# Values' products of two heads on the two halves of the array, and low halves of weights moved from GpSimd to VectorE

## The chip, the cores and the metric

One core of a Trainium2 chip runs the whole kernel. The time is that of the device for one execution, in microseconds (us), from several runs; the profile is of one more execution. TensorE multiplies matrices (its weight loads are shown as an engine of their own, PEld), VectorE (DVE) and ScalarE (ACT) work on vectors, GpSimd (POOL) does too, and SyncE (SP) issues most of the DMAs.

## The reference

A token sequence (256 tokens, width 1024, float32) goes through two layers of a first block and one layer of a second. Each layer of the first block is a gated feed-forward network, a mixer and a second feed-forward network, with residual sums:

```
x = x + 0.5 * swiglu(rmsnorm(x, ffn1_norm[l]), ffn1_wg[l], ffn1_wu[l], ffn1_wd[l])
h = rmsnorm(x, mix_norm[l]) @ w_in[l]
h_a, h_b, h_c = jnp.split(h, [A_COLS, A_COLS + B_COLS], axis=-1)
o = concatenate([mla_mixer(h_a, ...), nsa_mixer(h_b, ...), diff_mixer(h_c, ...)])
x = x + o @ w_out[l]
x = x + 0.5 * swiglu(rmsnorm(x, ffn2_norm[l]), ffn2_wg[l], ffn2_wu[l], ffn2_wd[l])
```

The mixer has six heads of latent attention (mla), six of sparse attention with three parts each (compressed blocks, selected, window; nsa) and four of differential attention (diff). A head has 64 columns of values. The second block projects the normed residual to z, xBC, dt and three streams of a short convolution, runs a state-space scan and the convolution, projects back, and ends in a mixture of 16 experts.

## The kernel before

**Precision in two halves.** Weights arrive in float32 in a tile `st`. `split` makes of each unit two pieces, and of each piece a high half `wh` (a rounded copy, by ScalarE, line 167) and a low half `wl = st - wh` (a subtraction, line 168). Its argument `lo` says for either piece who subtracts: "v" is VectorE, "p" is GpSimd. `LOW`, and a small table in `w_in_groups`, name the units with a "p". The activations are split in the same way (`xhl`, `uhl`, `ohl`, `hx`), and each product is three: high by high, low by high, high by low. Plain float32 products appear in the trace as two matmul records each.

**The order of work.** The program is written in the order of the formulas, with explicit orders where it matters (`ORDER` in the mixers: w for units of w_in, mp, np, dp for the preparation of the three kinds of heads, m, n, d for the heads, df for the end of diff; `PART2` for the second block). A planner at build time then sets the order of instructions on each engine from its own costs; each engine takes its instructions strictly in that order, and the semaphores are the planner's. `behind(i)` queues the instructions of a block that run on `i`'s engine behind `i`.

**The mixer.** After the last feed-forward product, `after` makes for each of four banks the operand `xhl` (lines 268, 269) and the sums of squares `sq` (lines 281 to 288). `_mixer` puts the sum over partitions on TensorE (`pss`), computes the inverse root `r`, and multiplies by the units of w_in. `mla_prepare` norms the latent vectors (`rq`, `ckvn`), transposes them (`ckvt`, `cqt`), and builds keys (`knope`, two heads at a time, side by side in 512 columns of 64 partitions) and queries. In `nsa_prepare` a small network compresses keys and values: h1, and from it `kcmp` and `vcmp`. A head then is: scores into a bank S, a softmax on VectorE and ScalarE (rows scaled on GpSimd or VectorE), transposes of the three blocks of the weights (`ptp`, copied to `PT`), and `pv`, the product with the values into a bank O. Two heads share a bank of O: the even head writes partitions 0 to 63, the odd one 64 to 127, so each product uses 64 of the array's 128 columns (`128*64` in the trace). An nsa head has three such products: selected (`hV`), compressed (`vcmp`, 15 rows) and window. At the end `wo` projects with eight products, each in a bank W, and two additions to `xT`.

**The second block.** `z_blocks` multiplies by z's columns, `norms` gives the two inverse roots as rows `rb`, `u_operand` makes the operand `uhl` from `xT` (three instructions for each k: u on VectorE, high half on ScalarE, low half on VectorE), `z_gates` applies the gate, `residual_norm` scales `xT`. Then `proj` multiplies by the units d, b0 to b3, x0 to x3 and those of the short convolution, and `conv` follows on ScalarE and VectorE.

**The experts** are computed in pairs of two: the products `gate`, `up` and `y` of one expert fill columns 0 to 63 of the array and those of the other 64 to 127, issued in turn.

Of the kernel before, what the change touches and what calls it, by code (L numbers as in the profile page):

```python
# [34 lines left out]
         "h0 s1 s1 g0 s1 s2 s2 n0 c1 h1 s2 s3 g1 n1 s3 c2 h2 g2 s3 "  # L35
         "| c3 h3 p5 g3 n2 y a w6 t0 t1 p7 t2 w0 n3 t3 % w1 p4 w5 w2 w4 p5 w3 w7")

LOW = {k: "pp" for k in ["d", "b0", "b1", "b2", "b3", "x0", "x1", "x2", "x3", "w6", "w1", "w3"]
       + [(1, 0, 0, 1), (1, 0, 1, 0)]}
LOW.update({k: "vp" for k in ["h3", "g2"]})  # L40
ORDER = "w01 w5 w2 mp m0 m1 w8 w3 w4 w6 np w7 dp m2 m3 d0 d1 n0 n1 d2 d3 n2 n3 n4 n5 m4 df m5"

# [1 line left out]
class Block:  # L44
# [272 lines left out]
    def _ffn(self, l, which, xops, after, extra):  # L317
# [27 lines left out]
        def gu(g, units):  # L345
            ps = []
            if g == 0 and not finish:

                ws = [w for u in units for w in self.split(u, "n")]
                ps = [self.bank(tag, "gu") for tag in "BBCC"]  # L350
                for k, i in ([(k, i) for k in range(4) for i in range(4)]
                             + [(k, i) for i in range(4) for k in range(4, KD)]):
                    self.mm2(ps[i], ws[i][0][:, k], ws[i][1][:, k], xhl[:, k], k == 0, k == KD - 1)
                return ps
            for i, u in enumerate(units):
                for f, (wh, wl) in enumerate(self.split(u, "n", LOW.get((which, l, g, i), "vv"))):
                    p = self.bank("BC"[i], "gu")
                    ps.append(p)
                    if finish and g == 0:

                        o = p[:, 0:T]
                        for n, (w, x) in enumerate(((wh, xh), (wh, xl), (wl, xh))):
                            for k in range(KD):
                                self.mm(p[:, T:2 * T] if n == 1 else o, w[:, k], x[:, k], n == k == 0, n == 2 and k == KD - 1)
                        continue
                    for k in range(KD):
                        self.mm2(p, wh[:, k], wl[:, k], xhl[:, k], k == 0, k == KD - 1)
            return ps
# [21 lines left out]
            return hx  # L390

        def down(g, hx, u):
            w = self.split(u, "k", LOW.get((which, l, g, 2), "vv"))
            for b in range(4):
                for j in range(2):
                    o = acc[b][:, j * T:(j + 1) * T]
                    c = (2 * b + j) * 128
                    for k in range(2):
                        wh, wl = w[k]
                        self.mm3(o, wh[:, 0, c:c + 128], wl[:, 0, c:c + 128], hx[:, k, 0], hx[:, k, 1],  # L400
                                 g == 0 and j == 0 and k == 0, g == NG - 1 and j == 1 and k == 1)
                if g == NG - 1:
                    xv = self.xT[:, 2 * b:2 * b + 2].rearrange("p j t -> p (j t)")
                    nc.vector.scalar_tensor_tensor(xv, acc[b], 0.25, xv, op0=OP.mult, op1=OP.add)  # L404
                    after(b)
# [107 lines left out]
    def _mixer(self, l, xops, after):  # L513
# [76 lines left out]

        def w_in_groups(ids):

            ws = [self.split(units[i], "k", {2: "pp", 3: "pp", 4: "vp", 5: "vp"}.get(i, "vv")) for i in ids]
            ps = [self.bank(tags.pop(0) if tags else "W", "win") for _ in ids]
            for k0 in range(KD):
                for k, i, t in ([(k0, i, t) for i in range(len(ids)) for t in range(2)] if len(ids) > 1 else
                                [(k, 0, k0) for k in range(KD)] if k0 < 2 else []):
                    w, p, n = ws[i], ps[i], units[ids[i]][2]
                    o = p[:, t * 256:t * 256 + n]
                    ts = slice(t * 128, (t + 1) * 128)  # L600
                    first = t == 0 and k == 0
                    last = t == 1 and k == KD - 1
                    wh, wl = (v[:, k % 4] for v in w[k // 4])
                    self.mm(o, xh[:, k, ts], wh, first, False)
                    self.mm(o, xh[:, k, ts], wl, False, False)
                    self.mm(o, xl[:, k, ts], wh, False, last)
            for i, p in zip(ids, ps):
                for dst, d, c, m in groups[i][1]:
                    for t in range(2):
                        src = p[:, t * 256 + c:t * 256 + c + m]  # L610
                        if isinstance(d, tuple):

                            o = dst[:, t, 0:384].rearrange("p (u c) -> p u c", c=64)[:, d[0] // 64::2][:, 0:d[1]]
                            src = src.rearrange("p (u c) -> p u c", c=64)
                        else:
                            o = dst[:, t, d:d + m]
                        ACT(o, src, scale=r[:, t:t + 1])


        def mla_prepare():  # L620
# [44 lines left out]
            for h in range(0, 6, 2):  # L665
                p = self.bank("S", "knope")
                for i in range(2):
                    self.mm(p[0:64, i * T:(i + 1) * T], wukv[:, h + i, 0:64], ckvT, i == 0, True)
                ACT(KT[0:64, h:h + 2], p[0:64].rearrange("p (i t) -> p i t", i=2))
                p = self.bank("T", "qtp")  # L670
                for i in range(2):
                    for t in range(2):
# [6 lines left out]
        def transposes(blocks, name):  # L679

            p = self.bank("T", name)
            n = len(blocks) * 128
            for i, b in enumerate(blocks):
                tr(p[:, i * 128:(i + 1) * 128], b, ident)
            s = ap.tile([128, 384], F32, name="PT", tag="PT", bufs=4)
            return p, s, n

        def store_o(c, p):
            ACT(oh[:, c], p)
            nc.vector.tensor_sub(ol[:, c], p, oh[:, c].bitcast(F32))  # L690

        opair = {}

        def pv(h, c0, pt, v, first, last):

            if h % 2 == 0 and first:
                opair[c0] = self.bank("O", "opair")
            p = opair[c0]
            o = p[(h % 2) * 64:(h % 2) * 64 + 64]
            self.mm(o[:, 0:256], v[0], pt[:, 0:256], first, False)  # L700
            self.mm(o[:, 128:256], v[1], pt[:, 256:384], False, last)

        def softmax(s, P, segs, gate=None, low=None):

# [34 lines left out]
        def mla_head(h):  # L739
# [4 lines left out]
            scale_rows(P, SEGS, softmax(s, P, SEGS), "m")  # L744
            p, pt, n = transposes(blocks(P), "ptp")
            (nc.vector.tensor_copy if h % 2 else nc.scalar.copy)(pt, p[:, 0:n])
            pv(h, h // 2, pt, [vm[:, t, h * 64:(h + 1) * 64] for t in range(2)], True, True)
            if h % 2:
                store_o(h // 2, opair[h // 2][:, 0:256])


        def nsa_prepare():
# [24 lines left out]
            for i in range(2):  # L777
# [4 lines left out]
            p, p2 = self.bank("T", "kcmp"), self.bank("S", "vcmp")  # L782
            vcmp = ap.tile([16, 128], F32, name="vcmp", tag="vcmp")
            for g in range(2):
                self.mm(p[g * 64:(g + 1) * 64, 0:15], w2[0:64], h1[0:64, 1, g * 15:(g + 1) * 15])
                self.mm(p2[0:15, g * 64:(g + 1) * 64], h1[64:128, 1, g * 15:(g + 1) * 15], w2[64:128], g == 0, True)
# [6 lines left out]
            for g in range(2):  # L793
                ACT(ks[g * 64:(g + 1) * 64, g, 0:15], p[g * 64:(g + 1) * 64, 0:15], scale=0.5)
            ACT(vcmp[0:15], p2[0:15, 0:128], scale=0.5)
# [11 lines left out]
            for g in range(2):  # L807
                q = slice(g * 64, (g + 1) * 64)
                nc.vector.tensor_copy(ks[q, g, 16:16 + T], p3[q, 0:256])
                nc.vector.tensor_copy(kw[q, g], p3[q, 256:512])  # L810

            th = ap.tile([128, 2, 18], F32, name="gth", tag="gth")
            nc.scalar.activation(th, hV[:, :, 384:402], AF.Tanh, scale=0.5)
# [10 lines left out]
        def nsa_head(h):  # L824
# [19 lines left out]
                tr(p2[0:16, t * 128:(t + 1) * 128], P[:, 384 + t * 16:400 + t * 16], ident)  # L844
            nc.vector.tensor_copy(cpt, p2[0:16, 0:T])
            vc = slice(128 + g * 64, 192 + g * 64)
            pv(h, 3 + h // 2, pt, [hV[:, t, vc] for t in range(2)], True, False)
            o = opair[3 + h // 2]
            self.mm(o[(h % 2) * 64:(h % 2) * 64 + 64, 0:256], vcmp[0:15, g * 64:(g + 1) * 64], cpt[0:15], False, False)
            s = self.bank("S", "S")  # L850
            scores(s, qt, kw[:, g], kw[:, g, 0:128])
            P = ap.tile([128, 384], F32, name="P", tag="P", bufs=6)
# [4 lines left out]
            pv(h, 3 + h // 2, pt, [hV[:, t, vc] for t in range(2)], False, True)  # L857
            if h % 2:
                store_o(3 + h // 2, o[:, 0:256])


# [86 lines left out]
        KO = [int(c) for c in "01345672"]  # L948
        wo = [self.cols(a["w_out"][l], (b * 256, b * 256 + 256)) for b in range(4)]
        for b in range(4):  # L950
            for j, (wh, wl) in enumerate(self.split(wo[b], "n", {}.get(b, "vv"))):
                p = self.bank("W", "wo")
                for k in KO:
                    self.mm2(p, wh[:, k], wl[:, k], ohl[:, k], k == KO[0], k == KO[7])
                xv = self.xT[:, 2 * b + j]
# [66 lines left out]
    def _part2(self, xops):  # L1022
# [80 lines left out]
        def u_operand():  # L1103
            for k in range(KD):
                u = ap.tile([128, T], F32, name="u", tag="q", bufs=4)
                nc.vector.scalar_tensor_tensor(u, self.xT[:, k], self.gfm[:, k:k + 1], rb[:, 1], op0=OP.mult, op1=OP.mult)
                ACT(uh[:, k, NM:], u)
                nc.vector.tensor_sub(ul[:, k, NM:], u, uh[:, k, NM:].bitcast(F32))  # L1108

        def residual_norm():  # L1110
            for k in range(KD):
# [282 lines left out]
        def run():  # L1394
            parts = decays()
            for name in steps:
                k, i = name[0], int(name[1:] or 0)
                if k == "z":
                    zs = z_blocks([int(c) for c in name[1:]])
                    if len(zs[0]) == 1:  # L1400
                        z_gates(*zs)
                elif k == "u":
                    norms()
                    u_operand()
                    z_gates(*zs)
                elif k == "r":
                    residual_norm()
                elif k == "d":
                    next(parts)
                elif k == "b":  # L1410
# [468 lines left out]
```

## Time and profile before

| | |
|---|---|
| median of 3 runs | 1592.82 us (1591.33 to 1594.35) |
| the profiled execution | 1591.45 us; its span, from first to last instruction, 1589.7 us |
| granted TensorE clock, mean | 0.984 |
| first feed-forward network of layer 0 | to 204 us |
| mixer of layer 0 | from 204 to some 350 us |
| mixer of layer 1 | from some 740 to 905 us |
| second block without experts | from 1089 to some 1340 us |

An engine is busy while it executes; TensorE's records overlap, so the time that a product holds the engine is read from start to start. A clock of 1.0 is 2.4 GHz and 0.5 is 1.2 GHz; a window between the two had some of each. In a row, `out<-in` names the tiles.

### The profile page before, as it was taken

Reading aid. Unit: us, or ns where it says so; the run is one execution under the profiler, and the core shown is the slowest. Engines: PE = TensorE matmul, PEld = TensorE weight load, DVE = VectorE, ACT = ScalarE, POOL = GpSimd, SP = SyncE. Lnnn points to the kernel's source line nnn. Section 1 sums busy time; section 2 is a strip of 40 time slices with the busy share of each in tenths; the row PEclk is TensorE's granted clock in tenths of the full one; section 3 lists DMA queues with packets and bytes.
Section 4 is the critical chain, followed back from the end, with each engine's and each line's share of the span. In section 5 each row is a group of like instructions: output and inputs, shape, how many; then the busy total and the mean of one; then the engine's idle time right before and its main releaser. Section 6 shows DMA issues by size and latency. Waiting matters only on the chain. (4 is left out here: it accounts for less than half of the span.)

```text
span 1589.7 us, 25210 instructions
## 1 busy us (share of the span) xinstructions
PE 1527.9 (96%) x9842; PEld 1266.7 (80%) x9842; DVE 1046.6 (66%) x1988; ACT 733.9 (46%) x1385; POOL 170.7 (11%) x174
## 2 busy tenths in 40 slices
PE   7999989999999999998999999999799999999996
PEld 6999988768999989998887799999799987444342
DVE  7777774868677786778467687778798875221122
ACT  5455455645554554455556455456554443010111
POOL 3000031330000000001115000001620122000000
PEclk9999999999999999999999999999899999999999
DMA  7756644205565555555440356555443479799993
GB/s 239 223 187 192 186 133 146 81 27 184 178 195 186 186 185 187 186 186 166 132 147 1 107 188 197 194 181 190 152 133 107 153 299 350 290 396 392 393 394 125
DMA packets 223557, 308.91 MB, mean 194 GB/s; under 512 B 20908, under 2 KB 167608, under 8 KB 223432
## 3 DMA queue, kind: packets, MB, share of 16 engines
q1 hardware_dynamic: 223128, 306.71, 57.8%
q8 instruction: 79, 1.29, 0.3%
q10 hardware_dynamic: 304, 0.53, 0.1%
q14 instruction: 46, 0.38, 0.1%
HBM read 306.16 MB, written 1.05 MB: 193 GB/s over the span
## 5 line engine op out<-in xcount | busy, mean ns | idle before, releaser
L167 ACT ACTIVATE wh<-st 128x1024 fp32r<-128x1024 f32 (+1 forms) x382 | 400.1, 1060 | 355.4 <-PE gu L99 116.8
L168 DVE TENSOR_TENSOR wl<-st,wh 128x1024 fp32r<-128x1024 f32 (+1 forms) x340 | 413.2, 1226 | 207.0 <-ACT wh L167 200.1
L99 PE MATMUL gu<-xhl,wh 128*128 128x512 f32 (+1 forms) x1440 | 492.1, 391 | 3.9 <-ACT wh L167 2.2
L99 PE MATMUL gu<-xhl,wl 128*128 128x256 f32 x1408 | 388.3, 279 | 0.0
L99 PEld LDWEIGHTS gu<-xhl,wh 128*128 128x128 f32 x1440 | 267.3, 189 | 63.1 <-ACT wh L167 3.5
L99 PEld LDWEIGHTS gu<-xhl,wl 128*128 128x128 f32 x1408 | 263.5, 189 | 0.1
L99 PE MATMUL acc<-hx,wh 128*128 128x256 f32 x1408 | 252.1, 281 | 0.0
L99 PEld LDWEIGHTS acc<-hx,wh 128*128 128x128 f32 x1408 | 216.2, 188 | 1.7
L168 POOL TENSOR_TENSOR wl<-st,wh 128x1024 fp32r<-128x1024 f32 (+1 forms) x42 | 102.6, 2461 | 1015.0 <-ACT wh L167 772.3
L99 PE MATMUL acc<-hx,wl 128*128 128x256 f32 x704 | 196.9, 281 | 0.0
L99 PE MATMUL proj<-uhl,wh 128*128 128x272 f32 (+2 forms) x592 | 131.0, 311 | 8.3 <-DVE uhl L1108 6.1
L99 PEld LDWEIGHTS acc<-hx,wl 128*128 128x128 f32 x704 | 132.6, 188 | 0.0
L99 PE MATMUL win<-wh,xhl 128*128 128x256 f32 (+1 forms) x576 | 111.1, 291 | 0.2 <-DVE xT L404 0.2
L99 PEld LDWEIGHTS proj<-uhl,wh 128*128 128x128 f32 x592 | 98.5, 196 | 13.7 <-DVE uhl L1108 6.8
L99 PE MATMUL proj<-uhl,wl 128*128 128x272 f32 (+2 forms) x328 | 96.5, 294 | 0.0
L99 PEld LDWEIGHTS win<-wh,xhl 128*128 128x128 f32 x576 | 93.5, 198 | 1.8 <-issue 1.1
L99 PE MATMUL win<-wl,xhl 128*128 128x256 f32 (+1 forms) x288 | 84.7, 294 | 0.0
L388 ACT ACTIVATE hx<-up 128x512 fp32r<-128x512 f32 x44 | 27.8, 632 | 94.3 <-DVE up L387 94.3
L99 PEld LDWEIGHTS proj<-uhl,wl 128*128 128x128 f32 x328 | 64.0, 195 | 0.2
L723 POOL TENSOR_SCALAR P<-P,mx 128x128 f32<-128x128 f32 (+2 forms) x88 | 54.3, 633 | 84.1 <-DVE mx L716 68.0
L99 PEld LDWEIGHTS win<-wl,xhl 128*128 128x128 f32 x288 | 56.9, 198 | 2.9 <-issue 2.7
L1776 DVE SCALAR_TENSOR_TENSOR ys<-y,rc,ys 128x512 fp32r<-128x512 f32 x16 | 11.7, 749 | 67.2 <-ACT ys L1593 66.8
(522 smaller groups left out, 2243.1 us busy)
## 6 DMA issues: line engine op xcount, KB each, us to landing
st<-ffn_wg SPq DMA_DIRECT2D x44, 1024.0 KB, 5.4
st<-ffn_wu SPq DMA_DIRECT2D x44, 1024.0 KB, 5.4
st<-ffn_wd SPq DMA_DIRECT2D x44, 1024.0 KB, 4.9
st<-w_in SPq DMA_DIRECT2D x36, 1024.0 KB, 5.4
st<-w_out SPq DMA_DIRECT2D x16, 1024.0 KB
mf<-expert_w_gate SPq DMA_DIRECT2D x25, 512.0 KB, 9.4
mf<-expert_w_down SPq DMA_DIRECT2D x21, 512.0 KB, 10.7
mf<-expert_w_up SPq DMA_DIRECT2D x18, 512.0 KB, 11.2
```

Source lines behind the costliest of these rows:

```text
L99: return self.nc.tensor.matmul(out, lhsT, rhs, start=start, stop=stop, skip_group_check=True)
L167: hi = self.nc.scalar.activation(hl[0], src, AF.Copy)
L168: sub = (self.nc.gpsimd if lo[i] == "p" else self.nc.vector).tensor_sub(hl[1], src, hl[0].bitcast(F32))
L388: nc.scalar.activation(hh, up, AF.Copy)
L723: (nc.gpsimd if key + str(i) in "c0 c1 c2 d0 d1 m0 w0 w1".split() else nc.vector).tensor_scalar(P[:, d], P[:, d], r[:, i:i + 1], None, op0 ...
L1776: V.scalar_tensor_tensor(yl, py[half], rc[:, 1:2], yh.bitcast(F32), op0=OP.mult, op1=OP.subtract)
```

## The change

- The product with the values is no longer issued with each head: `pv` puts the head's `PT` aside, and behind the odd head `pv_pair` issues both heads' products, first both of 256 columns, then both of 128, to the two column halves in turn. The compressed products of an nsa pair follow the selected ones. The bank O is taken by the odd head. `PT` has five buffers for four.
- `knope` puts two heads on the two column halves (partitions 0 to 63 and 64 to 127), and two copies take them out, one on ScalarE, one on VectorE.
- `kcmp` and `vcmp` move behind the transposes of queries and keys.
- `LOW` keeps b3, x0 to x3 ("pp") and h3, g2 ("vp"). The low halves of d, b0 to b2, w1, w3, w6, of a gate and an up unit at the start, and of six pieces of w_in in each mixer go from GpSimd to VectorE: 30 of 42.
- `wo` takes its banks from W and S in turn.
- In the second block, the VectorE instructions of `z_gates` and `residual_norm` stand behind the last low half of `u_operand`.

```diff
-LOW = {k: "pp" for k in ["d", "b0", "b1", "b2", "b3", "x0", "x1", "x2", "x3", "w6", "w1", "w3"]
-       + [(1, 0, 0, 1), (1, 0, 1, 0)]}
+LOW = {k: "pp" for k in ["b3", "x0", "x1", "x2", "x3"]}
 LOW.update({k: "vp" for k in ["h3", "g2"]})
...
-            ws = [self.split(units[i], "k", {2: "pp", 3: "pp", 4: "vp", 5: "vp"}.get(i, "vv")) for i in ids]
+            ws = [self.split(units[i], "k") for i in ids]
...
                 for i in range(2):
-                    self.mm(p[0:64, i * T:(i + 1) * T], wukv[:, h + i, 0:64], ckvT, i == 0, True)
-                ACT(KT[0:64, h:h + 2], p[0:64].rearrange("p (i t) -> p i t", i=2))
+                    self.mm(p[i * 64:(i + 1) * 64, 0:T], wukv[:, h + i, 0:64], ckvT)
+                for i in range(2):
+                    (nc.vector.tensor_copy if i else nc.scalar.copy)(KT[0:64, h + i], p[i * 64:(i + 1) * 64, 0:T])
...
-            s = ap.tile([128, 384], F32, name="PT", tag="PT", bufs=4)
+            s = ap.tile([128, 384], F32, name="PT", tag="PT", bufs=5)
...
-        def pv(h, c0, pt, v, first, last):
-
-            if h % 2 == 0 and first:
-                opair[c0] = self.bank("O", "opair")
-            p = opair[c0]
-            o = p[(h % 2) * 64:(h % 2) * 64 + 64]
-            self.mm(o[:, 0:256], v[0], pt[:, 0:256], first, False)
-            self.mm(o[:, 128:256], v[1], pt[:, 256:384], False, last)
+        waiting = {}
+
+        def pv(key, pt, v):
+
+            waiting.setdefault(key, []).append((pt, v))
+
+        def pv_pair(o, key, first, last):
+
+            two = list(zip((o[0:64], o[64:128]), waiting.pop(key)))
+            for o_, (pt, v) in two:
+                self.mm(o_[:, 0:256], v[0], pt[:, 0:256], first, False)
+            for o_, (pt, v) in two:
+                self.mm(o_[:, 128:256], v[1], pt[:, 256:384], False, last)
...
-            pv(h, 3 + h // 2, pt, [hV[:, t, vc] for t in range(2)], True, False)
-            o = opair[3 + h // 2]
-            self.mm(o[(h % 2) * 64:(h % 2) * 64 + 64, 0:256], vcmp[0:15, g * 64:(g + 1) * 64], cpt[0:15], False, False)
+            pv("s", pt, [hV[:, t, vc] for t in range(2)])
+            waiting.setdefault("c", []).append((cpt, vcmp[0:15, g * 64:(g + 1) * 64]))
+            if h % 2:
+                o = self.bank("O", "opair")
+                pv_pair(o, "s", True, False)
+                for i, (c, v) in enumerate(waiting.pop("c")):
+                    self.mm(o[i * 64:(i + 1) * 64, 0:256], v, c[0:15], False, False)
...
-                p = self.bank("W", "wo")
+                p = self.bank("WS"[j], "wo")
...
-                nc.vector.tensor_sub(ul[:, k, NM:], u, uh[:, k, NM:].bitcast(F32))
+                low_u = nc.vector.tensor_sub(ul[:, k, NM:], u, uh[:, k, NM:].bitcast(F32))
+            return low_u.ins
...
                 elif k == "u":
                     norms()
-                    u_operand()
-                    z_gates(*zs)
+                    done = u_operand()
+                    with self.behind(done):
+                        z_gates(*zs)
                 elif k == "r":
-                    residual_norm()
+                    with self.behind(done):
+                        residual_norm()
```

## Rows read from the trace of the kernel before

**Rows 1.** The page's first part: busy time, share and instructions of each engine.

```profile
PE 1527.9 (96%) x9842; PEld 1266.7 (80%) x9842; DVE 1046.6 (66%) x1988; ACT 733.9 (46%) x1385; POOL 170.7 (11%) x174
```

**Rows 2.** TensorE's waits: for whom, us in total, times, the longest.

```profile
PE pss L99 <- DVE sq L288: 9.2, 2, 4.8
PE proj L99 <- DVE uhl L1108: 6.1, 3, 3.8
...
PE acc L99 <- DVE rr L131: 2.6, 1, 2.6
...
PE wo L99 <- DVE xT L957: 1.9, 2, 0.9
PE kcmp L99 <- DVE h L780: 1.8, 2, 0.9
PE ckvt L641 <- DVE ckvn L634: 1.8, 2, 0.9
```

**Rows 3.** VectorE in order of time, head of the first mixer: start, us, instructions.

```profile
207.83 0.88 DVE L269 SCALAR_TENSOR_TENSOR xhl<-xT,v,xhl 128x256 fp32r<-128x256 f32 x2
208.62 0.69 DVE L286 TENSOR_TENSOR sq<-sq 128x512 f32<-128x512 f32 x1
209.23 5.17 DVE L269 SCALAR_TENSOR_TENSOR xhl<-xT,v,xhl 128x256 fp32r<-128x256 f32 x2
214.31 2.82 DVE L286 TENSOR_TENSOR sq<-sq 128x512 f32<-128x512 f32 x1
```

**Rows 4.** GpSimd in order of time, the same stretch.

```profile
208.89 7.70 POOL L168 TENSOR_TENSOR wl<-st,wh 128x1024 fp32r<-128x1024 f32 x3 [183.45 <-ACT wh L167]
```

**Rows 5.** Windows: engines' busy us (instructions), granted clock, DMA share, GB/s.

```profile
217.00:225.00 8.00, 7.35 (x36) 7.35 (x37) 2.91 (x15) 1.49 (x3) 0.00 (x0) 0.57 0.51 131
...
290.00:337.00 47.00, 45.72 (x305) 33.31 (x303) 38.60 (x167) 31.64 (x139) 26.38 (x43) 1.00 0.11 35
...
1113.00:1134.00 21.00, 14.36 (x82) 13.39 (x81) 16.32 (x28) 9.57 (x19) 10.69 (x4) 0.76 0.42 133
...
1134.00:1200.00 66.00, 60.87 (x477) 58.77 (x476) 59.12 (x111) 36.15 (x68) 25.61 (x11) 0.97 0.48 144
```

**Rows 6.** The page's costliest groups: the low halves on VectorE and on GpSimd.

```profile
L168 DVE TENSOR_TENSOR wl<-st,wh 128x1024 fp32r<-128x1024 f32 (+1 forms) x340 | 413.2, 1226 | 207.0 <-ACT wh L167 200.1
...
L168 POOL TENSOR_TENSOR wl<-st,wh 128x1024 fp32r<-128x1024 f32 (+1 forms) x42 | 102.6, 2461 | 1015.0 <-ACT wh L167 772.3
```

**Rows 7.** TensorE in order of time, among the nsa heads.

```profile
310.85 0.86 PE L99 MATMUL opair<-PT,hV 128*64 128x256 f32 x4
311.65 0.55 PE L684 MATMUL ptp<-ident,P 128*128 128x128 f32 x3
312.12 0.64 PE L99 MATMUL opair<-cpt,vcmp 15*64 15x256 f32 x2
```

**Rows 8.** The tile `opair`: its matmul records, min/median/max ns, forms.

```profile
L99 PE MATMUL opair<-PT,hV x96: 272/326/431, 310.9 to 878.8; 128*64 128x256 f32 x48, 128*64 128x128 f32 x48
...
L99 PE MATMUL opair<-PT,vm x48: 272/326/431, 269.5 to 882.3; 128*64 128x256 f32 x24, 128*64 128x128 f32 x24
...
L99 PE MATMUL opair<-cpt,vcmp x24: 374/400/425, 312.1 to 877.4; 15*64 15x256 f32 x24
```

**Rows 9.** TensorE in order of time, two experts' products `y`.

```profile
1405.25 0.64 PE L99 MATMUL y<-ms,acts 128*64 128x512 f32 x1
1405.25 0.64 PE L99 MATMUL y<-mh,acts 128*64 128x512 f32 x1
1405.73 0.59 PE L99 MATMUL y<-ms,acts 128*64 128x512 f32 x1
```

**Rows 10.** TensorE in order of time, keys of the mla heads.

```profile
249.78 1.08 PE L99 MATMUL knope<-ckvT,wm 128*64 128x256 f32 x4
```

**Rows 11.** VectorE in order of time, the second block's operand.

```profile
1108.66 4.10 DVE L1106 SCALAR_TENSOR_TENSOR u<-xT,gfm,rb 128x256 f32<-128x256 f32 x4
...
1127.89 0.75 DVE L1108 TENSOR_TENSOR uhl<-u,uhl 128x256 fp32r<-128x256 f32 x2
```

More of the change, by code (lines that the diff above doesn't have):

```diff
@@ L355, in gu @@
             for i, u in enumerate(units):
-                for f, (wh, wl) in enumerate(self.split(u, "n", LOW.get((which, l, g, i), "vv"))):
+                for f, (wh, wl) in enumerate(self.split(u, "n", "vv")):
                     p = self.bank("BC"[i], "gu")
@@ L392, in down @@
         def down(g, hx, u):
-            w = self.split(u, "k", LOW.get((which, l, g, 2), "vv"))
+            w = self.split(u, "k", "vv")
             for b in range(4):
@@ L690, in store_o @@
             nc.vector.tensor_sub(ol[:, c], p, oh[:, c].bitcast(F32))
-        opair = {}
-        def pv(h, c0, pt, v, first, last):
-            if h % 2 == 0 and first:
-                opair[c0] = self.bank("O", "opair")
-            p = opair[c0]
-            o = p[(h % 2) * 64:(h % 2) * 64 + 64]
-            self.mm(o[:, 0:256], v[0], pt[:, 0:256], first, False)
-            self.mm(o[:, 128:256], v[1], pt[:, 256:384], False, last)
+        waiting = {}
[7 more added lines that the diff above has]
+                self.mm(o_[:, 128:256], v[1], pt[:, 256:384], False, last)
         def softmax(s, P, segs, gate=None, low=None):
@@ L746, in mla_head @@
             (nc.vector.tensor_copy if h % 2 else nc.scalar.copy)(pt, p[:, 0:n])
-            pv(h, h // 2, pt, [vm[:, t, h * 64:(h + 1) * 64] for t in range(2)], True, True)
+            pv("m", pt, [vm[:, t, h * 64:(h + 1) * 64] for t in range(2)])
             if h % 2:
-                store_o(h // 2, opair[h // 2][:, 0:256])
+                o = self.bank("O", "opair")
+                pv_pair(o, "m", True, True)
+                store_o(h // 2, o[:, 0:256])
         def nsa_prepare():
@@ L781, in nsa_prepare @@
                                                op0=OP.add, op1=OP.mult)
[L782 to L786, printed above, removed]
             ks = ap.tile([128, 2, 16 + T], F32, name="ks", tag="hA")
@@ L792, in nsa_prepare @@
             nc.gpsimd.memset(kw, 0.0)
-            for g in range(2):
-                ACT(ks[g * 64:(g + 1) * 64, g, 0:15], p[g * 64:(g + 1) * 64, 0:15], scale=0.5)
-            ACT(vcmp[0:15], p2[0:15, 0:128], scale=0.5)
             qT = ap.tile([128, 3, T], F32, name="qT", tag="qT")
@@ L810, in nsa_prepare @@
                 nc.vector.tensor_copy(kw[q, g], p3[q, 256:512])
+            p, p2 = self.bank("T", "kcmp"), self.bank("S", "vcmp")
+            vcmp = ap.tile([16, 128], F32, name="vcmp", tag="vcmp")
+            for g in range(2):
+                self.mm(p[g * 64:(g + 1) * 64, 0:15], w2[0:64], h1[0:64, 1, g * 15:(g + 1) * 15])
+                self.mm(p2[0:15, g * 64:(g + 1) * 64], h1[64:128, 1, g * 15:(g + 1) * 15], w2[64:128], g == 0, True)
+            for g in range(2):
+                ACT(ks[g * 64:(g + 1) * 64, g, 0:15], p[g * 64:(g + 1) * 64, 0:15], scale=0.5)
+            ACT(vcmp[0:15], p2[0:15, 0:128], scale=0.5)
             th = ap.tile([128, 2, 18], F32, name="gth", tag="gth")
@@ L846, in nsa_head @@
             vc = slice(128 + g * 64, 192 + g * 64)
-            pv(h, 3 + h // 2, pt, [hV[:, t, vc] for t in range(2)], True, False)
-            o = opair[3 + h // 2]
-            self.mm(o[(h % 2) * 64:(h % 2) * 64 + 64, 0:256], vcmp[0:15, g * 64:(g + 1) * 64], cpt[0:15], False, False)
+            pv("s", pt, [hV[:, t, vc] for t in range(2)])
+            waiting.setdefault("c", []).append((cpt, vcmp[0:15, g * 64:(g + 1) * 64]))
+            if h % 2:
+                o = self.bank("O", "opair")
+                pv_pair(o, "s", True, False)
+                for i, (c, v) in enumerate(waiting.pop("c")):
+                    self.mm(o[i * 64:(i + 1) * 64, 0:256], v, c[0:15], False, False)
             s = self.bank("S", "S")
@@ L856, in nsa_head @@
             vc = slice(256 + g * 64, 320 + g * 64)
-            pv(h, 3 + h // 2, pt, [hV[:, t, vc] for t in range(2)], False, True)
+            pv("w", pt, [hV[:, t, vc] for t in range(2)])
             if h % 2:
+                pv_pair(o, "w", False, True)
                 store_o(3 + h // 2, o[:, 0:256])
@@ L950, in _mixer @@
         for b in range(4):
-            for j, (wh, wl) in enumerate(self.split(wo[b], "n", {}.get(b, "vv"))):
-                p = self.bank("W", "wo")
+            for j, (wh, wl) in enumerate(self.split(wo[b], "n")):
+                p = self.bank("WS"[j], "wo")
                 for k in KO:
@@ L1400, in run @@
                     if len(zs[0]) == 1:
-                        z_gates(*zs)
+                        with self.behind(done):
+                            z_gates(*zs)
                 elif k == "u":
                     norms()
-                    u_operand()
-                    z_gates(*zs)
+                    done = u_operand()
+                    with self.behind(done):
+                        z_gates(*zs)
                 elif k == "r":
-                    residual_norm()
+                    with self.behind(done):
+                        residual_norm()
                 elif k == "d":
```

## The prediction

> **What bounds the kernel now.** The page's first part comes first: TensorE is busy 96% of the span, VectorE 66%, ScalarE 46%, GpSimd 11% [rows 1]. So a product that vanishes from TensorE's queue is worth about its own time, and the rest of the time is in TensorE's waits. I read next the list of those waits, longest in total first [rows 2]. Six of its lines concern code of this change: `pss` (9.2 us, once in each mixer), `proj` for `uhl` (6.1), `acc` for `rr` (2.6, start), `wo` (1.9), `kcmp` (1.8) and `ckvt` (1.8). Five of them wait for VectorE. Why is an engine with a third of its time free late?
>
> The order of time on VectorE at the head of the first mixer answers it [rows 3]. Two `xhl` instructions took 0.88 us together from 207.83, the next two of the same form 5.17 from 209.23; a `sq` add of 128x512 took 0.69 at 208.62 and 2.82 at 214.31. In that time GpSimd was in three low-half subtractions, from 208.89 for 7.70 us [rows 4]. VectorE's instructions there end about when GpSimd's do: each was held until the other engine's subtraction was over. Held in this way: 4.3 + 2.1 = 6.4 us, and behind them stood `pss`, for which TensorE waited 4.4 (of its 9.2 the longer wait, 4.8, is the other mixer's). The price goes on afterwards: from 217 to 225 us the granted clock was 0.57 in the mean, that is mostly the lower level of 1.2 GHz, while TensorE was fully fed [rows 5]. Of 8 us that is some 3.4 lost.
>
> So a low half on GpSimd costs 2461 ns there and, when VectorE wants to work beside it, up to two more us on VectorE; on VectorE it costs 1226 ns [rows 6].
>
> **The change, part by part.** *Pairs of heads.* One head's product with the values is four matmul records (the two of 256 columns, then the two of 128). One such group holds TensorE from 310.85 to the next work at 311.65, 0.80 us; a compressed one's 0.64 of busy, less the same overlap of 0.06, is 0.58 [rows 7]. The records number 96 + 48 and 24, that is 36 and 12 groups [rows 8]: 36 x 0.80 + 12 x 0.58 = 35.8 us. Now two heads go out together, to column halves 0-63 and 64-127. What that costs, this trace shows in the experts, which already do it: the two halves' `y` products start together at 1405.25, and the next of the first half at 1405.73 [rows 9]. Two records of 128x512 thus take the time of one. A pair then costs what a head cost, and 17.9 us leave TensorE's queue. The lower bound is that halves follow one another: then only the gaps at either end of a group are saved, at most 0.15 of 0.80, some 3 us. I take concurrency.
>
> A rule speaks against it. The Trainium skill, "TensorE: Matmul & The Clock Gate", Part 3 on packing small matmuls, says that a weight load overlaps a running matmul only where the row group differs; the halves here share all rows, so by it the second half would load after the first half's matmul and the sum would lose the 17.9 but for some 3. The experts' rows disagree.
>
> How much of 17.9 reaches the end? The heads' stage is nearly even between engines: from 290 to 337 us TensorE was busy 45.7 and VectorE 38.6 of 47 [rows 5]. Six pairs of values and three compressed ones lie in the nsa heads, one pair in the last mla heads: 7 x 0.80 + 3 x 0.58 = 7.3 us less for TensorE, which would leave 39.7 to VectorE's 38.6. The highest share that VectorE holds in any stretch shown is 59.1 of 66, 90% [rows 5]. At 90% the stage takes 42.9, a gain of 4.1, not 7.3. The other two pairs of a mixer (1.6) lie where VectorE has more air. Per mixer 5.7; the second mixer's heads are the same. I allow 13 for both, a little over 2 x 5.7, since win products can fill in; bounds 4 and 17.9. The fifth `PT` buffer costs only memory; it holds the waiting head's weights, and the chain of an odd head has other heads' products to hide under.
>
> *`knope` on two halves.* Four records in 1.08 us [rows 10], six times; two together leave about 0.65. Gain 0.43 x 6 = 2.6, less for the copy that is now two, one of them on VectorE (6 x 0.4 us, beside w_in products). I take 2; bounds 1 and 2.6.
>
> *Low halves to VectorE.* 42 lay on GpSimd [rows 6]; 12 remain there (b3, x0 to x3, half of h3 and g2), 30 move: VectorE gets 30 x 1.23 = 37 us (two of d's are half as long). It loses the times for which it was held. At the mixers' heads the three that move belong to w5 and w2. If all three came before the last add, 3 x 1.23 = 3.7 would replace 6.4: `pss` would be 2.7 sooner and TensorE would wait 1.7 instead of 4.4; if none, nothing. I take 0.6. Gain per mixer: about 3.9 of wait and the clock's 3.4, since a clock that fell behind a wait of four us need not fall behind one of half a us. 14 for both; bounds 7 and 16 (9.2 + 6.8). Each moved subtraction also frees its `st` buffer, so the loads on SP's queue behind it start when VectorE gets to it; with 1.23 against 2.46 us that is sooner, unless VectorE's queue is long.
>
> At the start the four GpSimd subtractions of the first two units hold the chain of `rr`; of 2.6 us wait I take 2 (bounds 1 and 2.6), as VectorE must now do these subtractions too. `ckvt` waits 1.8 behind two more: take 1.6.
>
> *Part 2's operand.* `u_operand` makes 8 u and 8 low halves. From rb's end VectorE begins at 1108.66; the last low half starts at 1127.89, with another ahead of it in that row [rows 11]. The first four u took 4.10 us, though two `xhl` of that size take 0.88 [rows 3]; the last two low halves took 0.75. Unheld, 16 x 0.42 is under 7 us: done by 1115.7, with three moved subtractions between (3.7) by 1119.4, which is 9 to 13 us before the present end at 1128.6. TensorE waits 6.1 for it in three places, so that shrinks to 0 to 2. That z's VectorE part and `residual_norm` now stand behind the last low half takes up to 16 instructions of about 0.42 out of the way; they are late next, beside the convolutions of b0 and b1. Between 1113 and 1134 TensorE was busy 14.4 of 21 at a clock of 0.76: 6.6 idle and 5.0 lost [rows 5]. The next 66 us have 5.1 idle, with VectorE at 90%, where the displaced 6.7 us and b0 to b2's 7.4 must fit. So I give a third back: 8 from 11.6. Bounds 3 and 18 (the later stretch's idle and clock too).
>
> *The rest.* `kcmp` moves behind ten transposes that need no h1: 1.8, take 1.6. The `wo` bank alternates between W and S, so the next product has not to wait for `xT`: 1.9, take 1.5.
>
> **Sum.** 13 + 2 + 14 + 2 + 1.6 + 8 + 1.6 + 1.5 = 43.7 off the profiled execution's 1591.45, which is 1.4 below the median of the runs shown: 1549 for a median.
>
> **The rivals.**
> 1. *VectorE becomes the bound.* For it: 82% in the heads, 90% after 1134. The pairs give 4, part 2 gives 3, the mixers' heads 7, the rest 5: 19, so 1574. Against: what it is spared is measured in us at each place.
> 2. *More falls away than I allow.* All upper bounds: 17.9 + 2.6 + 16 + 2.6 + 1.8 + 18 + 1.8 + 1.9 = 62.6, so 1530. For it: TensorE is fed from other heads; against: VectorE's share.
> 3. *The halves run one after another.* 13 + 2 becomes 3: 1561. Against it stand the experts' rows; for it that their matmuls are 512 columns wide and these 256 and 128.
> 4. *Slower: pairs wait for the odd head.* An even head's product is not issued before the odd one's transposes, and TensorE takes its queue in order. If TensorE stands idle at each of the 24 pairs, the gain of 43.7 is gone from 1.8 us a pair; at three times a product, 2.4, it is 57.6, so 1607. Against: the pair stands where the odd head's own product stands today, behind the same chain, and no line of the waits is of `opair`.
>
> **How the numbers follow.** Forecast 0.56, rival 1 0.20, rival 2 0.13, rival 3 0.06, rival 4 0.03; 0.02 for gains and losses that happen to cancel. The likeliest alone spans 1537 to 1560. The range for 8 in 10 goes from rival 2's 1530 to rival 1's 1574. Within 0.2% (3.2 us) a measurement of this kernel can't tell a change from none. Faster 0.95, within it 0.02, slower 0.03.
>
> **What the next profile would show.** GpSimd's L168 at 12 instructions, VectorE's at 370; `xhl` instructions at 0.5 us at the mixers' heads, `pss` with hardly a wait, clock 1.0 behind it. `opair` records of two halves starting together, about 18 us less of them. The last `uhl` low half within 11 us of `rb`. VectorE's share in the heads near 90%. Wrong would be: `opair` starts 0.2 us apart; TensorE waiting for `PT` or `S`; `pss` still waiting behind VectorE's own L168; convolutions of b0 to b2 late by what was gained.

## The result and the profile after

The changed kernel took 1569.59 us in the median of four runs (1568.98 to 1572.28), the kernel before 1592.63 beside it: ratio 0.9858, 95% interval 0.9841 to 0.9875. That is 23.0 us less, where 43.7 were forecast. The sign was right and the time lies in the range, near its slow end, where the first rival stood and not the forecast.

The page's first part answers to [rows 1], the list of TensorE's waits to [rows 2] (engine, line, tile, who is waited for: us in total, times, longest).

```profile
span 1567.5 us, 25184 instructions
## 1 busy us (share of the span) xinstructions
PE 1514.2 (97%) x9842; PEld 1256.1 (80%) x9842; DVE 1035.7 (66%) x2024; ACT 731.1 (47%) x1385; POOL 96.5 (6%) x144
```

```profile
PE gu L98 <- DVE xT L967: 11.0, 4, 3.5
PE proj L98 <- DVE cv L1208: 5.1, 2, 4.2
PE xtp L208 <- DMA xtok<-x: 4.9, 1, 4.9
...
PE vcmp L98 <- DVE h L785: 1.8, 2, 0.9
```

The waits that the prediction wanted gone are gone: `pss`, `proj` for `uhl`, `acc` for `rr`, `wo`, `ckvt` (the view lists none of them). In their place stand 11.0 us of `gu` (the second feed-forward network's first products) for `xT`, and 5.1 of `proj` for a convolution. `kcmp` has moved, but `vcmp`, which moved with it, waits the same 1.8.

The low halves by engine answer to [rows 6] (instructions, then busy us and mean ns of one):

```profile
L167 POOL TENSOR_TENSOR wl<-st,wh 128x1024 fp32r<-128x1024 f32 x12 | 29.5, 2462 | 365.0 <-ACT wh L166 357.8 <-DVE dv L1168 5.3 <-DVE cv L1208 1.9
L167 DVE TENSOR_TENSOR wl<-st,wh 128x1024 fp32r<-128x1024 f32 (+1 forms) x370 | 447.5, 1219 | 209.4 <-ACT wh L166 198.6 <-PE qp L98 5.4 <-PE h L98 4.6
```

VectorE has 36 instructions more, the 30 low halves and six copies of `knope`, and yet is busy 1035.7 us for 1046.6, since a held instruction counts as busy [rows 3]. Where it was held in the kernel before [rows 3, 4] it now takes 474 ns for each `xhl`, by line and form from 200 to 212 us:

```profile
L167 DVE TENSOR_TENSOR wl<-st,wh 128x1024 fp32r<-128x1024 f32 x4 | 4.9, 1214 | 0.0
L268 DVE SCALAR_TENSOR_TENSOR xhl<-xT,v,xhl 128x256 fp32r<-128x256 f32 x7 | 3.1, 474 | 0.0
L285 DVE TENSOR_TENSOR sq<-sq 128x512 f32<-128x512 f32 x3 | 2.0, 681 | 0.0
```

Windows of the changed kernel, to be set against [rows 5] (columns: stretch, its length and TensorE's busy time, weight loads, VectorE, ScalarE, GpSimd, granted clock, DMA share, GB/s):

```profile
206.00:217.00 11.00, 11.00 (x96) 11.00 (x96) 8.27 (x21) 4.79 (x7) 0.00 (x0) 1.00 0.74 195
217.00:225.00 8.00, 8.00 (x69) 8.00 (x69) 4.63 (x10) 7.05 (x22) 0.00 (x0) 1.00 0.58 171
290.00:337.00 47.00, 46.71 (x299) 33.10 (x299) 28.10 (x117) 21.64 (x90) 20.80 (x35) 1.00 0.01 2
348.00:356.00 8.00, 2.66 (x11) 1.75 (x10) 8.00 (x16) 3.83 (x7) 0.00 (x0) 0.77 0.85 269
875.00:884.00 9.00, 3.30 (x15) 2.39 (x14) 9.00 (x17) 4.28 (x8) 0.00 (x0) 0.85 0.88 277
1094.00:1115.00 21.00, 15.97 (x116) 15.56 (x116) 19.56 (x33) 12.30 (x23) 7.64 (x3) 0.88 0.72 225
```

The mixer's head is what was forecast: TensorE busy throughout, clock 1.00. The surprise is 348 to 356 and 875 to 884, a mixer's end in each layer: VectorE is busy 100%, TensorE a third, and the clock falls. The times of some records tell where the gain came and went (us from the trace: the end of the last `wo`, the start of the first record otherwise; a feed-forward network ends where the mixer's first product starts):

```
                              before   after   difference
end of first feed-forward      204.7   200.4    -4.3
first S of mixer 0             259.3   247.8   -11.4
last wo of mixer 0             367.4   348.2   -19.2
mixer 1's first product        740.2   728.5   -11.7
first S of mixer 1             793.4   775.4   -18.0
last wo of mixer 1             903.0   875.8   -27.2
first zp of the second block  1088.7  1069.9   -18.8
first gate of the experts     1359.4  1334.0   -25.4
end                           1589.7  1567.5   -22.2
```

Both mixers win, and behind each of them 7.5 and 8.4 us are handed back.

**Why VectorE is late at the mixer's end.** VectorE in order of time there in the changed kernel (start, length, engine and line; in brackets what a wait was for), then TensorE:

```profile
346.91 1.22 DVE L167 TENSOR_TENSOR wl<-st,wh 128x1024 fp32r<-128x1024 f32 x1
348.05 0.48 DVE L268 SCALAR_TENSOR_TENSOR xhl<-xT,v,xhl 128x256 fp32r<-128x256 f32 x1
348.44 1.22 DVE L167 TENSOR_TENSOR wl<-st,wh 128x1024 fp32r<-128x1024 f32 x1
349.58 0.42 DVE L966 TENSOR_TENSOR xT<-wo,xT 128x256 f32<-128x256 f32 x1
...
351.83 0.42 DVE L967 TENSOR_TENSOR xT<-wo,xT 128x256 f32<-128x256 f32 x1
...
355.36 0.41 DVE L967 TENSOR_TENSOR xT<-wo,xT 128x256 f32<-128x256 f32 x1
```

```profile
347.90 0.28 PE L98 MATMUL wo<-ohl,wl 128*128 128x256 f32 x1
348.01 0.39 PE L98 MATMUL gu<-xhl,wh 128*128 128x512 f32 x1
...
352.40 0.76 PE L98 MATMUL gu<-xhl,wh 128*128 128x512 f32 x1 [3.53 <-DVE xT L967]
...
355.19 0.77 PE L98 MATMUL gu<-xhl,wh 128*128 128x512 f32 x1 [1.81 <-DVE xT L967]
```

With five banks in place of two (W has two, S three), TensorE is through `wo` at 348.2, but the additions to `xT` go on to 355.8, mixed with the next network's low halves of 1.22 us each. The network's products need all of `xT`. The same record of 512 columns takes 0.39 before that wait and 0.76 behind it: the clock's lower level.

**How the pairs went out.** TensorE in order of time in the changed kernel; the number behind the x counts the matmul records of a group:

```profile
258.32 0.87 PE L98 MATMUL opair<-PT,vm 128*64 128x256 f32 x8
...
320.54 0.86 PE L98 MATMUL opair<-PT,hV 128*64 128x256 f32 x6
321.34 0.39 PE L849 MATMUL ptc<-ident,P 128*16 128x128 f32 x2
...
322.77 0.65 PE L98 MATMUL opair<-PT,hV 128*64 128x256 f32 x2
323.34 0.50 PE L98 MATMUL wo<-ohl,wh 128*128 128x512 f32 x1
```

A whole pair is eight records in one group, as at 258.32. At 322.77 only the even head's two records of 256 columns stand, which the planner pulled ahead (0.57 to the next work), and the other six follow later (0.80, as at 320.54). In each mixer one pair of nine is whole; the other eight cost 1.37 for 0.80, and the six products of the compressed part 0.57 each instead of two together. By these durations the products take 16 x 1.37 + 2 x 0.80 + 12 x 0.57 = 30.4 us: of the 17.9 that should leave TensorE's queue 5.4 left it.

### The profile page after: what moved, and what is told of

Same layout as the page of the kernel before. It is cut to its first block, busy times and chain, and to the rows that moved or that the text cites. A ratio compares the mean times of both kernels' runs of the same rounds, so it can differ in the third digit from the quotient of the medians.

```text
span 1567.5 us, 25184 instructions
## 1 busy us (share of the span) xinstructions
PE 1514.2 (97%) x9842; PEld 1256.1 (80%) x9842; DVE 1035.7 (66%) x2024; ACT 731.1 (47%) x1385; POOL 96.5 (6%) x144
## 4 chain that ended last, share of the span: by engine, by line
PE 91%; DVE 6%; ACT 1%; issue 1%; DMA 0%; POOL 0%; ACTq 0%; DVEq 0%
PE gu L98 32%; PE acc L98 16%; PE proj L98 7%; PE win L98 6%; PE gate L98 4%; PE y L98 4%; PE up L98 4%; PE h L98 3%; PE S L98 3%; PE opair L98 2%; PE wo L98 2%; PE zp L98 1%; DVE wl L167 1%; PE moe L98 1%; PE ptp L684 1%; PE xgp L98 1%
## 5 line engine op out<-in xcount | busy, mean ns | idle before, releaser
L167 DVE TENSOR_TENSOR wl<-st,wh 128x1024 fp32r<-128x1024 f32 (+1 forms) x370 | 447.5, 1219 | 209.4 <-ACT wh L166 198.6
L716 ACT ACTIVATE P<-S,mx 128x256 f32<-128x256 f32 (+2 forms) x128 | 48.8, 396 | 17.5 <-DVE mx L712 4.4
```

Source lines behind the costliest of these rows:

```text
L167: sub = (self.nc.gpsimd if lo[i] == "p" else self.nc.vector).tensor_sub(hl[1], src, hl[0].bitcast(F32))
L716: nc.scalar.activation(P[:, d], s[:, c], AF.Exp, bias=m[:, 0, i:i + 1], accum_out=m[:, 1, i:i + 1])
```

## The experiments

All ran beside the kernel before, which had medians of 1593.98, 1593.07 and 1594.17 us in the three groups below. Intervals are 95%.

### First group: the banks of `wo`, the order of a pair, the low halves

`wo_w`: the changed kernel, `wo` from the two banks W alone again.

```diff
-                p = self.bank("WS"[j], "wo")
+                p = self.bank("W", "wo")
```

> The changed kernel with wo's banks taken from W alone, as before the change. Theory: with five banks wo's products run ahead of their additions, VectorE gets them in a bunch and the first product of the second feed-forward network stands waiting for xT; without the S banks the waits of gu for xT (11.0 us) and the low clock behind them (6.8 us twice at half, 6.8 lost) go, and wo's own two waits (1.9) come back: 1569.6 - 11.0 - 6.8 + 1.9 = 1554. Rival, VectorE is the bound of the mixer: its work is the same, so the wait only moves, 1567 to 1571.

Measured: 1555.66 us, ratio 0.9767 (0.9749 to 0.9784), 13.9 less than the changed kernel. `gu` waits no more for `xT`, and the window of the mixer's end is full at a clock of 1.00 with VectorE at 78%:

```profile
348.00:356.00 8.00, 7.97 (x47) 6.73 (x46) 6.22 (x10) 3.75 (x7) 0.00 (x0) 1.00 0.71 234
```

```profile
346.78 0.42 DVE L966 TENSOR_TENSOR xT<-wo,xT 128x256 f32<-128x256 f32 x1 [0.17 <-PE wo L98]
347.24 0.42 DVE L967 TENSOR_TENSOR xT<-wo,xT 128x256 f32<-128x256 f32 x1
347.81 1.22 DVE L167 TENSOR_TENSOR wl<-st,wh 128x1024 fp32r<-128x1024 f32 x1
...
350.01 0.42 DVE L967 TENSOR_TENSOR xT<-wo,xT 128x256 f32<-128x256 f32 x1
```

VectorE follows each product at once, with one low half between, and the last addition starts 0.5 us behind the end of the last product (349.5 to 350.0), not 7 (348.2 to 355.4). The two banks, whose wait of 0.9 per mixer [rows 2] the change removed, had kept the two engines in step. The theory is confirmed as far as the banks go: 1554 was expected. What the run doesn't part is the number of banks and the planner's order on VectorE, which changes with it. With five banks five additions, 2.1 us of work, stand behind 348.2 with three low halves and other work between them; whether five banks with the additions put first would be as good as two was not tried.

`tight`: the changed kernel, with the odd head's 256 columns first and the other three products queued behind them, so that nothing can be pulled ahead; the compressed products likewise.

```diff
...
+            lead = self.mm(ob[:, 0:256], vb[0], pb[:, 0:256], first, False)
+            with self.behind(lead.ins):
+                self.mm(oa[:, 0:256], va[0], pa[:, 0:256], first, False)
+                self.mm(ob[:, 128:256], vb[1], pb[:, 256:384], False, last)
+                self.mm(oa[:, 128:256], va[1], pa[:, 256:384], False, last)
...
```

> The changed kernel with each pair issued as one piece: the odd head's product of 256 columns first, the other three queued behind it; the compressed products in the same way. Theory: the planner had pulled the even head's first product ahead in nearly all pairs, so opair costs TensorE 33.8 us and not 20; kept together it costs 20 to 21, and of the 13 us some 8 reach the end: 1561 (1557 to 1566). Rival, VectorE is the bound of the heads: TensorE's saving turns into waits for S and PT, 1567 to 1571.

Measured: 1556.99 us, ratio 0.977 (0.9754 to 0.9785), 12.6 less than the changed kernel, at the near edge of the range expected. The wait for `xT` stays (11.1 us).

`wo_w_tight`: both edits.

> Both at once. Theory: the two losses are separate and add up, 1554 - 8 = 1546, near the prediction's 1549. Rival, VectorE is the bound: 1565 to 1571.

Measured: 1543.68 us, ratio 0.969 (0.9674 to 0.9705): the two add up (25.9 less than the changed kernel, of 13.9 + 12.6). TensorE among its nsa heads:

```profile
309.89 0.87 PE L98 MATMUL opair<-PT,hV 128*64 128x256 f32 x8
310.69 0.55 PE L684 MATMUL ptp<-ident,P 128*128 128x128 f32 x3
311.17 0.65 PE L98 MATMUL opair<-cpt,vcmp 15*64 15x256 f32 x4
311.75 0.44 PE L684 MATMUL ptp<-ident,P 128*128 128x128 f32 x2
```

Eight records hold TensorE 0.80 us, to the hundredth what four did in [rows 7], and four compressed ones 0.58. All 18 pairs are whole, and the products take 17.9 us in the two mixers together, where 35.8 stood. Two halves of the columns cost the time of one, with weights that are loaded into the same rows. The rule that the prediction took from the Trainium skill ("TensorE: Matmul & The Clock Gate", Part 3: a load overlaps a running matmul only in another row group), taken alone, would have made this 1.6, twice the 0.80; the measurement decides against it for column halves.

`low_only`: the kernel before with the 30 low halves moved to VectorE and nothing else.

```diff
-LOW = {k: "pp" for k in ["d", "b0", "b1", "b2", "b3", "x0", "x1", "x2", "x3", "w6", "w1", "w3"]
-       + [(1, 0, 0, 1), (1, 0, 1, 0)]}
+LOW = {k: "pp" for k in ["b3", "x0", "x1", "x2", "x3"]}
...
-            ws = [self.split(units[i], "k", {2: "pp", 3: "pp", 4: "vp", 5: "vp"}.get(i, "vv")) for i in ids]
+            ws = [self.split(units[i], "k") for i in ids]
```

> The kernel before, with nothing of the change but the low halves moved to VectorE. Theory: the low halves alone remove the waits of pss (9.2) with the clock behind them (6.8), the waits at the start (3.3) and of ckvt (1.8), and shorten the operand of the second block: 1592.6 - 21 to 1592.6 - 26, so 1567 to 1572. Rival, VectorE is the bound and 37 us more work on it costs what the freed holds give: 1585 to 1593.

Measured: 1561.32 us, ratio 0.9806 (0.9789 to 0.9823), 32.7 less than before. It beats the expectation, and it beats the whole change by 8.3: what else the change does cost more than it brought. From `low_only` to `wo_w` (all but the banks) lie 5.7, from there to the changed kernel the banks' 13.9 the other way.

### Second group: what the low halves are worth in place, and part 2

`low_undone`: the changed kernel with the 30 low halves back on GpSimd (the diff of `low_only`, reversed).

> The changed kernel with the 30 low halves of weights back on GpSimd; pairs, knope, kcmp, the banks of wo and the order of part 2 as changed. Theory (the low halves carry the gain and the parts add up): the kernel before with the low halves alone took 1561.3, that is 32.7 less than before and 8.3 less than the changed kernel, so the rest of the change costs 8: some 1602, slower than before; pss waits 8 to 9 us in all again, with the clock at half behind it. Rival (the pairs also spare VectorE's held stretches, so that both parts overlap): 1580 to 1590.

Measured: 1594.87 us, ratio 1.0007 (0.9998 to 1.0016). No difference from before, between the two expectations. `pss` waits 9.1 and `gu` for `xT` 11.5. The rest of the change, as issued, is worth nothing alone. If the banks cost the 13.9 here too, the other edits bring 12 here against 5.7 beside the moved low halves, and the parts overlap by some 6 us; no run shows the banks' price here.

`free`: `wo_w_tight` without the order in part 2 (no `behind(done)`). `best`: `wo_w_tight` with no low half on GpSimd at all. `free_allv`: both.

```diff
...
-                    with self.behind(done):
-                        z_gates(*zs)
+                    z_gates(*zs)
...
-                    with self.behind(done):
-                        residual_norm()
+                    residual_norm()
```
```diff
-LOW = {k: "pp" for k in ["b3", "x0", "x1", "x2", "x3"]}
-LOW.update({k: "vp" for k in ["h3", "g2"]})
+LOW = {}
```

> wo_w_tight (1543.7) without the order behind the last low half of u in part 2: the VectorE instructions of z's gates and of the residual scaling are free again. Theory (the gates, late and then held by GpSimd, make the convolution of b0 late, for which TensorE waits 4.2 us with the clock at half behind it, 3.4 of it at full price lost): 1538 to 1541. Rival (the order buys the uhl waits, 6.1 us before, and without it they come back): 1545 to 1550.

> wo_w_tight (1543.7) with the last 12 low halves of weights on VectorE too, none on GpSimd. Theory (what still holds VectorE, and so z's gates and the convolution of b0, are the three subtractions of b3 and x0 on GpSimd from 1105 to 1113): the held instructions there go, TensorE's wait of 4.2 for cv goes, 1536 to 1541. Rival (VectorE is at 90% from 1115 to 1180, and 12 more subtractions of 1.22 us make it the bound there): 1546 to 1552, the wait moves to later convolutions.

> Both: wo_w_tight without the order in part 2 and with no low half on GpSimd. Theory of the held gates: the two remedies meet the same wait, so together no more than the better of them, 1536 to 1541. Rival of VectorE as the bound: 1546 to 1552.

Measured: 1542.04 (ratio 0.9679, 0.9665 to 0.9692), 1545.26 (0.9701, 0.9688 to 0.9715) and 1544.29 us (0.9693, 0.9679 to 0.9706). The intervals of all three overlap with that of `wo_w_tight`: neither edit is worth what can be told apart. All three lie above what the theory gave (1541 at most), `best` and `free_allv` a little under its rival's 1546. So the theory behind them fell. It was that GpSimd's three subtractions hold z's gates and so the convolution of b0. In the changed kernel the gates are held, while GpSimd subtracts:

```profile
1104.14 0.76 DVE L1106 SCALAR_TENSOR_TENSOR z<-zth,z 128x256 f32<-128x256 f32 x2
...
1107.30 3.76 DVE L1106 SCALAR_TENSOR_TENSOR z<-zth,z 128x256 f32<-128x256 f32 x2 [0.76 <-ACT zth L1105]
1110.98 1.02 DVE L1208 SCALAR_TENSOR_TENSOR cv<-proj,v,cv 128x270 f32<-128x270 f32 x2
```

```profile
1105.63 7.64 POOL L167 TENSOR_TENSOR wl<-st,wh 128x1024 fp32r<-128x1024 f32 x3 [260.21 <-ACT wh L166]
```

In `best` no gate is held, and TensorE waits just as long:

```profile
1076.34 3.25 DVE L1125 SCALAR_TENSOR_TENSOR xT<-xT,v,rb 128x256 f32<-128x256 f32 x8
1079.51 0.76 DVE L1108 SCALAR_TENSOR_TENSOR z<-zth,z 128x256 f32<-128x256 f32 x2
1080.18 2.36 DVE L166 TENSOR_TENSOR wl<-st,wh 128x1024 fp32r<-128x1024 f32 x2
1082.45 0.50 DVE L1210 SCALAR_TENSOR_TENSOR cv<-proj,v,cv 128x271 f32<-128x271 f32 x1
```

```profile
PE proj L97 <- DVE cv L1210: 4.2, 1, 4.2
```

The convolution comes behind the displaced `residual_norm`, gates and low halves. In `free` this wait is gone, and others have come (among them 2.3 for `uhl`) without a change in the end. So the order displaces a wait, as the prediction said of what is late next; how much of VectorE's work could go elsewhere wasn't tried.

### Third group: single terms

`pairs_only`: the kernel before with the pairs alone, issued as in `tight` (and the fifth `PT` buffer). `low_pairs`: the same with the 30 low halves moved. `win_only`: the kernel before with only the w_in pieces of the mixers on VectorE (the second hunk of `low_only`). `db_only`: the kernel before with only d, b0, b1 and b2 on VectorE.

```diff
-LOW = {k: "pp" for k in ["d", "b0", "b1", "b2", "b3", "x0", "x1", "x2", "x3", "w6", "w1", "w3"]
+LOW = {k: "pp" for k in ["b3", "x0", "x1", "x2", "x3", "w6", "w1", "w3"]
```

> The kernel before with the pairs alone (products of the odd head's 256 columns first, the other three behind it), low halves as before. Theory (the term of 13 was right for pairs that go out whole, with opair at 20 us of TensorE): 13 to 15 less than before, 1578 to 1580. Rival (while GpSimd still holds VectorE in the heads, VectorE sets the pace there and the pairs give little alone): 1586 to 1591.

> The kernel before with the pairs as in tight and the 30 low halves on VectorE, nothing else of the change. Theory (of the 17.6 that lie between low_only, 1561.3, and wo_w_tight, 1543.7, the pairs make 13 to 15): 1546 to 1548; the remainder of 3 to 4 is knope, kcmp and vcmp's place. Rival (the pairs make all of it, the other edits nothing): 1543 to 1545.

> The kernel before with the six pieces of w_in of each mixer alone on VectorE. Theory by the prediction's terms (mixers' heads 14, ckvt 1.6): 1577 to 1579, pss without a wait and a clock of 1.0 behind it. Rival (the held time of VectorE costs in other places of the mixer too, since low_only gained more than the terms for low halves, 14 + 2 + 1.6 + 8 = 25.6 against 32.7): 1571 to 1575.

> The kernel before with the low halves of d, b0, b1 and b2 alone on VectorE (part 2), its order as before. Theory by low_only's milestones (7.1 gained between z's last block and the scan, 9 to the router): 1584 to 1586. By the prediction's term (8): 1585. Rival (VectorE, at 90% after 1134, can't take the 10 us and the gain is given back by the end): 1589 to 1592.

Measured:

```
             median us   ratio to before (95%)       less than before
pairs_only    1572.32    0.9867 (0.9851 to 0.9883)    21.9
low_pairs     1545.22    0.9690 (0.9673 to 0.9708)    49.0
win_only      1576.36    0.9892 (0.9877 to 0.9908)    17.8
db_only       1586.67    0.9954 (0.9940 to 0.9968)     7.5
```

`pairs_only` is better than either theory: 21.9, more than the 17.9 that I had counted as TensorE's. `low_pairs` lies 16.1 below `low_only`; its time is between the two expectations, 0.2 us from the rival's, by which the pairs make all of it and the other edits nothing. `win_only` lies between the two theories (its gain, 17.8, reaches the least that the rival gave, 17.6 from 1592.6). `db_only` is within 0.7 us of the first theory. In `pairs_only` the window that answers to the heads has VectorE at 38.45 of 45, 85%, and TensorE still at 97%:

```profile
290.00:335.00 45.00, 43.48 (x333) 32.84 (x332) 38.45 (x165) 30.72 (x137) 26.00 (x43) 1.00 0.05 14
```

## Why the prediction came out as it did

**Right in mechanism, and somewhat low in size.** *Low halves on GpSimd hold VectorE, and the clock falls behind the wait.* The terms for the mixers' heads and `ckvt` were 14 + 1.6; `win_only` gives 17.8. From 217 to 225 us the clock went from 0.57 [rows 5] to 1.00. The start was given 2 and measures 4.3. In all the low halves bring 32.7 where 14 + 2 + 1.6 + 8 = 25.6 stood; six of the 30, those of w1, w3 and w6, had no term, and no run has them alone. (All six waits that the prediction lists are for VectorE, not five; no term hangs on it.)

Part 2's 8 was for its low halves and the order together. `db_only` gives 7.5 without the order, so the low halves are the whole of it. The order did shorten the operand as forecast: the last `uhl` starts 20.3 us behind `rb`'s start in the kernel before, 15.6 in `db_only`, 10.9 in the changed kernel:

```profile
1089.10 0.69 DVE L1080 COPY rb<-rbb 128x512 f32<-128x512 f32 x1
...
1099.97 0.42 DVE L1118 TENSOR_TENSOR uhl<-u,uhl 128x256 fp32r<-128x256 f32 x1
```

But by `free` these last 4.7 us bring nothing at the end. That the term came out is in this part luck.

The Trainium skill ("SBUF — State Buffer", Who interferes with whom) has GpSimd and VectorE share a pair of ports under an exclusive lock. The rows agree: two gates take 3.76 us while GpSimd subtracts, and 0.76 when it doesn't.

**Failed: the pairs' term of 13.** Its premise, that a pair costs what a head cost, is right for a pair that goes out whole (0.80 for eight records). The step that failed is that the pairs go out as they are written. The planner moved the even head's first product ahead in 16 of 18 pairs, and 5.4 of 17.9 us left TensorE. All edits but the banks and the low halves (pairs, `knope`, `kcmp` and part 2's order) together brought 5.7; the terms had 13 + 2 + 1.6.

**And mis-sized the other way.** The reduction from 17.9 to 13, with VectorE at 90% as the limit, was not needed: whole pairs brought 16.1 with the low halves moved and 21.9 without. The traces say where. From the first S to the end of the last `wo` the kernel before takes 108.2 and 109.6 us in its two mixers and `pairs_only` 100.0 and 100.3, 17.5 less together: TensorE's 17.9 reaches the end nearly whole. (`low_only` takes 104.5 and 103.8 there, `low_pairs` 96.0 and 96.7: 15.6.) Of the rest, 1.5 lie before the first S of mixer 0, and the two profiled executions are 19.7 apart where the medians are 21.9, a difference within the spread of the runs.

**Failed: the `wo` banks' term of 1.5.** I priced it as a wait removed, with nothing on the other side. It cost 13.9: two waits in each layer (3.5 and 1.8; 3.5 and 2.2) and the lower clock behind them. Rival 1, VectorE as the bound, was the right kind of thing at the wrong place: it gave 1574, near the time measured, but put the loss in the heads and after 1134, not where `wo` ends.

**Small.** `knope`, `kcmp`, part 2's order and the rest lie between `low_pairs` (1545.2) and `wo_w_tight` (1543.7): not to be told from nothing, where 3.6 stood for the first two. Rivals 3 and 4 are out: halves run together, and among the changed kernel's waits none is of `opair`. Rival 2 had a point that the sum hid: low halves and whole pairs alone bring 49.0 (`low_pairs`), more than the 43.7 forecast for everything.

**The account.** Low halves -32.7, pairs and small edits as issued -5.7, banks +13.9: -24.5, against -23.0 measured. The three are steps of one chain, from the kernel before over `low_only` and `wo_w` to the changed kernel, so they add up by themselves; the 1.5 is the kernel before, 1593.98 in one group and 1592.63 in the other. That the time lay in the range owes something to luck too: what the low halves brought beyond their terms, 7, made up for a part of what the pairs and the banks lacked. From the first `gate` to the end the changed kernel takes 233.5 us for 230.3, in code that the change doesn't touch. The excess goes with the moved low halves (232.6 in `low_only`, but 230.4 in `pairs_only` and 230.3 in `low_undone`); its cause is open.

With the two W banks for `wo` and whole pairs, `wo_w_tight` (1543.7) and `free` (1542.0) beat both kernels: 3.1 to 3.2% less than before. `low_pairs` (1545.2), with fewer edits, is as good within the intervals.

## What to carry to other kernels

A shortage of banks that makes an engine wait 0.9 us may be what keeps producer and consumer in step; before easing it, look at what the consumer has queued for the moment when everything arrives at once. Where a planner orders the instructions, a gain that needs several of them side by side has to be tied together, and the trace's record counts show whether it was. Of two engines that slow each other, it can pay to move the work to the busier one if it does it in half the time: here VectorE took 30 subtractions more and its busy time fell, as the held time went.

## What was not expected of the hardware

Of the chip, little: both points below were counted on from other rows [rows 3, 9], and these runs add the sizes. Two gates of 128x256 took 3.76 us beside a GpSimd subtraction and 0.76 without: about 1.5 us on each instruction of 0.38. And two column halves cost no more than one: eight records in 0.80 us, four in 0.80. What was not expected is the price of more banks, told above.
